# Two gate chunks in front of the first query pairs, and attention blocks two chunks later

## The chip, the cores and the metric

The kernel runs on one core of a Trainium2 chip. The metric is the device time of one execution in microseconds (us); the lower, the better. Engines are named as in the profile: PE (TensorE, the matmuls), DVE (VectorE), ACT (ScalarE), POOL (GpSimd) and SP (the queue that issues most DMAs).

## The reference

One decoder layer on 512 tokens of width 1024, in float32: a SwiGLU block, a mixer, and a second SwiGLU block, each between two RMS norms. The change lies in the mixer:

```
z = u @ w_in
gate_br, x_br, q, k, v, g_lru, g_attn = jnp.split(z, IN_SPLITS, axis=-1)
xc = causal_depthwise_conv(x_br, conv_w, conv_b)
y_lru = rg_lru(xc, ...) * jax.nn.gelu(gate_br)
q, k = apply_rope(q, cos, sin), apply_rope(k, cos, sin)
y_attn = sliding_window_attention_with_sinks(q, k, v, attn_sinks)
merged = sigmoid(g_lru) * (y_lru @ w_proj_lru) + sigmoid(g_attn) * (y_attn @ w_proj_attn)
return merged @ w_out
```

`rg_lru` computes two gates of `xc` by small block-diagonal matrices and then runs a linear recurrence along the tokens. Attention has 16 query heads in 4 groups, one key/value head for each group, and a window of 128 tokens, so a block of 128 queries sees 256 keys (128 in the first block).

## The kernel before, in words

Each float32 operand of a matmul is split into a rounded high part and the low remainder, and a product is three matmuls (`mm3`, lines 133 to 135): high by high, high by low, low by high. A chunk is 128 output columns for all 512 tokens over 8 steps of the inner dimension (`feat_chunk`), so 24 matmuls of 128x512.

Weights go through one pipeline in the order of the list `worder`, 84 pieces of 128x1024. `wload` issues a DMA on SP's queue into a `wraw` tile (line 96). `wsplit` casts it on ACT into the high half of a `w` tile (line 103) and has DVE subtract for the low half (line 104). `wget` hands out the next tile and first has everything up to two pieces further on split; a split issues the load of the piece three further on. `w` tiles come from the pool `big`, 19 slots of 128x2048 floats; `wraw` tiles and the attention scores come from a pool of 8.

The order of the instructions on each engine is the work of the framework's scheduler: it takes the program's order as priority and fills by its own estimate of times. What the kernel writes is therefore the priority, and engines then run their queues strictly in the planned order. Side work is written as generators: `start` runs one up to its first `yield n`, and each `tick()`, at the end of every chunk, counts down; after n ticks the generator goes on.

The mixer's first part runs in this order:

- `v_group` and `x_group(0)`, `k_pair`, `x_group(1)`: the recurrent branch's columns in two groups of four chunks. Each chunk starts `lru_chunk`: convolution on DVE (L907), and some ticks later the gate matmuls (tiles `r` and `i`), activations on ACT, and DVE's products. The last chunk of a group does the tail for all four: L929 (DVE), a square root on ACT (L930), and one tick apart for each chunk L933 (a product) and L934 (the scan along the tokens). The scans leave the recurrence's result in `lm`, which `hl` lists.
- Query pairs 0 and 1, `q_pair(0)` and `q_pair(1)`: two chunks each (`rope_pair`), then the rotary step: four products on DVE (L990), two sums on POOL (L991, L992), two casts on ACT (L996) and two subtractions on DVE (L997). One tick later the result goes to DRAM (L1015), another tick later it comes back in another layout as `qt` (L1020).
- Eight gate chunks, `gate_chunk(c)`: Square and Tanh on ACT (L1086, L1088), three passes on DVE (L1087, L1089, L1090, the last with `hl`), then the split into `ylh` and `yll` (L1092 on ACT, L1093 on DVE). Chunks 0 to 3 need the first group's recurrence, 4 to 7 the second's.
- Query pairs 2 and 3.

Attention is cut into blocks `attend(g, n)`, g the group of heads and n the block of queries. A block starts with the scores (tile `at..b`, L1036), DVE's masking (L1037), the maximum (L1042) and small operations (L1043 to L1052), exponentials on ACT (L1049), and POOL's scaling (L1053). Four ticks later come transposes (L1059), casts (L1061) and subtractions (L1062), two ticks after that the product with the values (L1069) and the write into `ya` (L1074). `next_attend` starts the next block of a list `todo`. The eight blocks of groups 0 and 1 are started one behind each of the gate chunks 2 to 7 (`ATT_GATES`) and one behind each of the two chunks of pair 2, through the argument `unit` of `rope_pair`.

After that follow eight steps of `sig_gate(c, yl, "gl")`, each a gate chunk (`glg`) and a projection chunk (`glp`), with the eight blocks of groups 2 and 3 started between them, and then the same for the attention branch (`gag`, `gap`) and the output projection.

Of the kernel before, what the change touches and what calls it, by code (L numbers as in the profile page):

```python
# [16 lines left out]
P = 128  # L17
# [2 lines left out]
TAIL = 7  # L20
JSTD = {"f1": 6, "f2": 4}
GC = 4
WARM = 8
LEAD = 3
PRODUCTS = (1, 2, 5, 6, 3, 7, 4)
FEATURE_LAG = {"b1": (4, 1), "b2": (3, 3, 3, 5)}
ATT_GATES = (2, 3, 4, 5, 6, 7)
T = 512
NT = T // P
D = 1024  # L30
KD = D // P
# [11 lines left out]
def hybrid_block_kernel(ctx, tc, x, xt, g1, w_first, gains, gu1, gs1, ds1, w_x, w_gate, w_q, w_k, w_v, w_gl, w_ga, w_pl, w_pa,  # L43
# [12 lines left out]
    def bank(name):  # L56
        return psum.tile([P, 512], F32, name=name, tag="bank")

    def t4(name, dtype=F32):
        return t4p.tile([P, 1024], dtype, name=name, tag="t4")  # L60

    def t2(name, dtype=F32):
        return t2p.tile([P, 512], dtype, name=name, tag="t2")

    def b8(name, shape, dtype=F32):
        return big.tile(shape, dtype, name=name, tag="b8")
# [4 lines left out]
    worder = []  # L71
    caps = []
    for gu in (gu1, gu2):
        worder += [gu[j, i] for j in range(gu.shape[0]) for i in range(2)]
        caps.append(len(worder))
        if gu is gu1:
            worder += [w_x[c] for c in range(4)] + [w_v[i] for i in range(2)] + [w_k[i] for i in range(2)]
            worder += [w_x[c] for c in range(4, 8)] + [w_q[i] for i in range(4)]
            worder += [w_gate[c] for c in range(8)] + [w_q[i] for i in range(4, 8)]
            worder += [w[c] for c in range(8) for w in (w_gl, w_pl)]  # L80
            worder += [w[c] for c in range(8) for w in (w_ga, w_pa)]
            worder += [w_o[c] for c in range(8)]
# [26 lines left out]
    def wget():  # L109
        i = wpos[0]  # L110
        wpos[0] += 1
        wsplit(i + 1 + AHEAD)
        return wready[i]
# [3 lines left out]
    def start(gen):  # L117
        n = next(gen, None)
        if n is not None:
            live.append([gen, n])  # L120

    def tick():
        for item in list(live):
            item[1] -= 1
            if item[1] <= 0:
                n = next(item[0], None)
                if n is None:
                    live.remove(item)
                else:
                    item[1] = n  # L130
# [22 lines left out]
    G.memset(idle.bitcast(F32), 0.0)  # L153
    for _ in range(WARM):
        PE.matmul(rb, lhsT=idle[:, :P], rhs=idle, start=True, stop=True)
# [21 lines left out]
    def feat_chunk(b, w, u, tok):  # L177
        wh, wl = w
        for k in range(KD):
            ks = slice(k * P, (k + 1) * P)  # L180
            mm3(b[:, tok], wh[:, ks], wl[:, ks], at(u, 0, k, tok), at(u, 1, k, tok), k == 0, k == KD - 1)
# [22 lines left out]
    def gate_up(u, name, first, fast, rs, ds, ending, also={}):  # L204
        ps = {}

        def pw(j):
            key = j // (2 * GC), j % 2
            if key not in ps:
                ps[key] = b8(f"{name}p{j}", [P, GC, T])  # L210
            return ps[key][:, j // 2 % GC, :]

# [179 lines left out]
    class Whole:  # L392
# [6 lines left out]
        def part(self, g, r, hi):  # L399
            n = GC if g < 2 else 3  # L400
            return self.ps[g, r][:, :n, 256:512] if hi else self.ps[g, r][:, :n, 0:256]
# [20 lines left out]
        def add_up(self, q):  # L422
# [4 lines left out]
            if s % 2 == 0 and i == 5:  # L427
                self.sums[g] = t4(f"{self.name}sum{g}").rearrange("p (c t) -> p c t", c=GC)[:, :GC if g < 2 else 3]
                self.sub(self.sums[g], self.part(g, 0, True), self.part(g, 1, True))
# [3 lines left out]
        def high(self, q):  # L433
# [9 lines left out]
            if s % 2 == 0:  # L443
                z = {1: (0, False), 2: (1, False), 3: (1, False), 4: (1, True), 7: (0, True)}.get(i)
                z = self.sums[g] if z is None else self.part(g, *z)
                a = b8(f"{self.name}a{i}{g}", [P, 2, GC, 256], F32R)[:, :, :GC if g < 2 else 3]
                self.a[i, g] = a, z
# [491 lines left out]
    def x_group(gi):  # L939
        a4, m4, bx4 = (b8(f"{n}{gi}", [P, 4, T]) for n in ("la", "lm", "lb"))  # L940
        hl.append(m4)
        cr = range(4 * gi, 4 * gi + 4)
        if gi == 0:
            first_four(u2, "x", lambda c, b: start(lru_chunk(c, b, a4, m4, bx4, c == cr[-1])), lambda: (next(vs), gates()))
        else:
            for c in cr:
                w = wget()
                b = bank(f"x{c}")
                feat_chunk(b, w, u2, ALL)
                tick()  # L950
                start(lru_chunk(c, b, a4, m4, bx4, c == cr[-1]))
# [26 lines left out]
    def rope_pair(name, unit=lambda: None):  # L978
        bs = []
        for i in range(2):  # L980
            w = wget()
            b = bank(f"{name}{i}")
            feat_chunk(b, w, u2, ALL)
            tick()
            unit()
            bs.append(b)
        ba, bb = bs
        m = [t2(f"{name}m{i}") for i in range(4)]
        for o, z, i in zip(m, (ba, ba, bb, bb), (0, 1, 0, 1)):
            V.tensor_tensor(out=o, in0=z, in1=cs[:, i, :], op=ALU.mult)  # L990
        G.tensor_tensor(out=m[0], in0=m[0], in1=m[3], op=ALU.subtract)  # L991
        G.tensor_tensor(out=m[2], in0=m[2], in1=m[1], op=ALU.add)  # L992
        st = b8(f"{name}st", [P, 4, T], F32R)
        for i, z in enumerate((m[0], m[2])):
            hi, lo = (st[:, 2 * i, :], st[:, 2 * i + 1, :]) if name == "kk" else (st[:, i, :], st[:, 2 + i, :])
            A.copy(hi, z)  # L996
            V.tensor_tensor(out=lo, in0=z, in1=hi.bitcast(F32), op=ALU.subtract)  # L997
        return st.bitcast(F32)
# [12 lines left out]
    def q_pair(m, unit=lambda: None):  # L1011
        st = rope_pair(f"q{m}", unit)
        yield 1
        dr = dram.tile([P, 4, T], F32, name=f"q_halves{m}")
        SP.dma_start(dr, st)  # L1015
        yield 1
        qt = b8(f"qt{m}", [P, 4, T], F32R)
        src = dr.rearrange("(i p) r t -> r p i t", i=4)
        for r in range(4):
            SP.dma_start(qt[32 * r:32 * r + 32].bitcast(F32), src[r])  # L1020
        qts[m] = qt
# [57 lines left out]
    def gate_chunk(c):  # L1079
        w = wget()  # L1080
        b = bank(f"gt{c}")
        feat_chunk(b, w, u2, ALL)
        if c % 4 == 0:
            yl.append((b8(f"ylh{c}", [P, 4, T], F32R), b8(f"yll{c}", [P, 4, T], F32R)))
        p = t2(f"gp{c}")
        A.activation(p, b, AF.Square)  # L1086
        V.scalar_tensor_tensor(out=p, in0=p, scalar=1.0 / GELU_C, in1=b, op0=ALU.add, op1=ALU.mult)  # L1087
        A.activation(p, p, AF.Tanh, scale=SQRT_2_PI * GELU_C)  # L1088
        V.scalar_tensor_tensor(out=p, in0=p, scalar=1.0, in1=b, op0=ALU.add, op1=ALU.mult)  # L1089
        V.scalar_tensor_tensor(out=p, in0=p, scalar=0.5, in1=hl[c // 4][:, c % 4, :], op0=ALU.mult, op1=ALU.mult)  # L1090
        yh, yo = yl[-1]
        A.copy(yh[:, c % 4, :], p)  # L1092
        V.tensor_tensor(out=yo[:, c % 4, :], in0=p, in1=yh[:, c % 4, :].bitcast(F32), op=ALU.subtract)  # L1093
        tick()
# [24 lines left out]
    kp = [b8(f"kp{i}", [P, 2, 2, T], F32R) for i in range(2)]  # L1119
    start(k_pair(kp))  # L1120
    x_group(1)
    for m in range(2):
        start(q_pair(m))
    y0 = b8("ya0", [P, 4, T])
    todo = [(g, n) for n in range(NT) for g in range(2)]

    def next_attend(*a):
        if todo:
            g, n = todo.pop(0)
            start(attend(g, n, kp, vt, y0 if g < 2 else y1))  # L1130

    for c in range(KD):
        gate_chunk(c)
        if c in ATT_GATES:
            next_attend()
    start(q_pair(2, next_attend))
    start(q_pair(3))
    y1 = b8("ya1", [P, 4, T])
    ya = []

    def split_y(src, name):
# [137 lines left out]
```

## Time and profile before

| | us |
|---|---|
| median of 3 runs | 1113.12 (1112.94 to 1113.57) |
| the profiled execution's own time | 1113.28 |
| its span, first to last instruction | 1111.5 |
| PE busy | 1099.9 |
| DVE busy | 898.4 |
| ACT busy | 597.2 |
| POOL busy | 97.9 |

The rows of the profile that are shown below give a line of the code, an engine, an operation and its tiles, written as output<-inputs with buffer numbers left out; then partitions x elements, how many there are, and times. In a timeline the first column is the start in us from the start of the span, the second the length, and brackets at the end give the time that the engine was idle just before and which instruction it then waited for. Rows of like instructions are merged. In a list of waits the numbers are us in total, times, and the longest.

### The profile page before, as it was taken

The page shows a single profiled execution, that of the slowest core. Times are in us where ns is not written, and L with a number is a line of the kernel's source. Part 1 is how long each engine was busy: PE and PEld are TensorE (multiplying, and loading weights), DVE is VectorE, ACT ScalarE, POOL GpSimd, SP SyncE. Part 2 cuts the span into 40 slices and gives each one's busy share as a digit, 9 for nine tenths or more (in the row PEclk, how much of TensorE's full clock was granted, in tenths as well). Part 3 has the DMA queues.
Part 4 walks back from the last instruction along what each step waited for, and adds up shares of the span by engine and source line. Part 5 has one row for each costly group of instructions (what it writes and reads, how often), then busy time and mean ns, then how long its engine had stood idle before and what let it go on. Part 6 is the DMA issues. An engine that isn't in the chain of part 4 may idle for free.

```text
span 1111.5 us, 16695 instructions
## 1 busy us (share of the span) xinstructions
PE 1099.9 (99%) x6550; PEld 981.5 (88%) x6550; DVE 898.4 (81%) x1266; ACT 597.2 (54%) x983; POOL 97.9 (9%) x100
## 2 busy tenths in 40 slices
PE   9999999999999999999999999999999999999997
PEld 7889999988889988787888888888999999998886
DVE  7999898889988799999777562546768889979877
ACT  7445554564665659567555351425435455457563
POOL 0000000012211011014022000000000000001310
PEclk9999999999999999999999999999999999999999
DMA  8223333498967264512822340533313333377973
GB/s 319 65 71 114 110 96 100 150 219 211 227 205 267 83 161 144 151 57 69 258 72 95 114 169 21 162 141 110 119 60 94 114 114 100 92 214 181 233 177 114
DMA packets 46079, 154.88 MB, mean 139 GB/s; under 512 B 5552, under 2 KB 5680, under 8 KB 45360
## 3 DMA queue, kind: packets, MB, share of 16 engines
q1 hardware_dynamic: 36496, 122.09, 34.4%
q0 software_dynamic: 6912, 23.07, 11.0%
q10 hardware_dynamic: 2592, 8.66, 2.1%
q8 instruction: 51, 0.84, 0.3%
q14 instruction: 28, 0.23, 0.1%
HBM read 142.26 MB, written 11.53 MB: 138 GB/s over the span
## 4 chain that ended last, share of the span: by engine, by line
PE 91%; DVE 7%; ACT 1%; issue 1%; DVEq 0%; POOL 0%; ACTq 0%; POOLq 0%
PE f2X L135 5%; PE f2X L134 5%; PE f2X L133 5%; PE f1X L135 5%; PE f1X L133 5%; PE f1X L134 5%; PE f1f L850 2%; PE f2Q L134 2%; PE f2Q L135 2%; PE f2Q L133 2%; PE f1Q L135 1%; PE f1Q L134 1%; PE f1Q L133 1%; PE glg L135 1%; PE glp L133 1%; PE glp L135 1%
## 5 line engine op out<-in xcount | busy, mean ns | idle before, releaser
L104 DVE TENSOR_TENSOR w<-wraw,w 128x1024 fp32r<-128x1024 f32 x84 | 104.2, 1274 | 16.8 <-ACT w L103 14.5
L103 ACT CAST w<-wraw 128x1024 fp32r<-128x1024 f32 x84 | 84.4, 1047 | 21.9 <-PE glp L135 6.0
L135 PE MATMUL f1X<-u1m,f1W 128*128 128x256 f32 x256 | 72.5, 283 | 0.0
L134 PE MATMUL f1X<-u1m,f1W 128*128 128x256 f32 x256 | 72.4, 283 | 0.0
L133 PE MATMUL f1X<-u1m,f1W 128*128 128x256 f32 x256 | 72.4, 283 | 0.0
L420 DVE TENSOR_TENSOR f2w<-f2b,f2w 128x1024 fp32r<-128x1024 f32 (+1 forms) x42 | 46.6, 1132 | 11.6 <-ACT f2w L442 11.6
L420 DVE TENSOR_TENSOR f1w<-f1b,f1w 128x1024 fp32r<-128x1024 f32 (+1 forms) x42 | 46.7, 1132 | 4.0 <-ACT f1w L442 4.0
L135 PEld LDWEIGHTS f1X<-u1m,f1W 128*128 128x128 f32 x256 | 49.1, 192 | 0.2 <-DVE f1W L275 0.2
L133 PEld LDWEIGHTS f1X<-u1m,f1W 128*128 128x128 f32 x256 | 49.1, 192 | 0.1
L134 PEld LDWEIGHTS f1X<-u1m,f1W 128*128 128x128 f32 x256 | 49.1, 192 | 0.1
L442 ACT CAST f1w<-f1b 128x1024 fp32r<-128x1024 f32 (+1 forms) x42 | 40.0, 979 | 11.5 <-PE f1Y L135 3.9
L442 ACT CAST f2w<-f2b 128x1024 fp32r<-128x1024 f32 (+1 forms) x42 | 39.8, 978 | 10.8 <-PE f2Y L135 3.9
L464 POOL DMA_DIRECT2D f1b<-in_ds_dram x24 | 20.9, 870 | 278.1 <-DVE f1w L420 270.1
L464 POOL DMA_DIRECT2D f2b<-in_ds_dram x24 | 20.9, 871 | 263.5 <-DVE f2w L420 261.1
L134 PE MATMUL f2Q<-u3m,f2W 128*128 128x256 f32 x144 | 40.8, 283 | 0.0
L134 PE MATMUL f2X<-u3m,f2W 128*128 128x256 f32 x144 | 40.8, 283 | 0.0
L135 PE MATMUL f2X<-u3m,f2W 128*128 128x256 f32 x144 | 40.8, 283 | 0.0
L135 PE MATMUL f2Q<-u3m,f2W 128*128 128x256 f32 x144 | 40.8, 283 | 0.0
L135 PE MATMUL f2X<-u3h,f2W 128*128 128x256 f32 x144 | 40.8, 283 | 0.0
L133 PE MATMUL f2Q<-u3m,f2W 128*128 128x256 f32 x144 | 40.8, 283 | 0.0
L134 PE MATMUL f2X<-u3l,f2W 128*128 128x256 f32 x144 | 40.8, 283 | 0.0
L133 PE MATMUL f2X<-u3m,f2W 128*128 128x256 f32 x144 | 40.7, 283 | 0.0
(809 smaller groups left out, 3946.7 us busy)
## 6 DMA issues: line engine op xcount, KB each, us to landing
f1b<-in_ds_dram POOLq DMA_DIRECT2D x20, 512.0 KB, 9.3
f2b<-in_ds_dram POOLq DMA_DIRECT2D x20, 512.0 KB, 9.4
f2L<-in_gs_dram SPq DMA_DIRECT2D x18, 512.0 KB, 3.5
f2R<-in_gs_dram SPq DMA_DIRECT2D x18, 512.0 KB, 4.4
wraw<-in_gu_dram SPq DMA_DIRECT2D x16, 512.0 KB, 5.7
f1L<-in_gs_dram SPq DMA_DIRECT2D x16, 512.0 KB, 3.5
f1R<-in_gs_dram SPq DMA_DIRECT2D x16, 512.0 KB, 4.4
f1b<-in_ds_dram SPq DMA_DIRECT2D x16, 512.0 KB, 5.0
```

The costliest lines, as they stand in the source:

```text
L103: A.copy(w[:, 0, :], raws[n])
L104: V.tensor_tensor(out=w[:, 1, :], in0=raws[n], in1=w[:, 0, :].bitcast(F32), op=ALU.subtract)
L133: PE.matmul(o, lhsT=ah, rhs=bh, start=start, stop=False, skip_group_check=reopen)
L134: PE.matmul(o, lhsT=ah, rhs=bl, start=False, stop=False, skip_group_check=reopen)
L135: PE.matmul(o, lhsT=al, rhs=bh, start=False, stop=stop, skip_group_check=reopen)
L420: V.tensor_tensor(out=o, in0=x0, in1=x1, op=ALU.subtract)
L442: A.copy(w[:, 0], self.w[i, s][1])
L464: G.dma_start(raw, self.ds[s, more][:, :n], accum_op=ALU.add)
L850: PE.matmul(bs[i], lhsT=lw[:, i * P:(i + 1) * P], rhs=rx, start=k == 0 and n == 0, stop=k == KD - 1 and n == 2)
```

## The change

The loop of gate chunks is cut in two. Chunks 0 and 1 (`GF = 2`) are computed right behind `x_group(1)`, ahead of the query pairs 0 and 1; the other six follow behind these pairs. The list of weights is reordered in the same way. Attention blocks now start behind the gate chunks 4 to 7 instead of 2 to 7, and behind all four chunks of the query pairs 2 and 3 instead of pair 2's two. The output tile `ya1` is created ahead of pair 2, and `ya0` ahead of the pairs 0 and 1.

```diff
+GF = 2
...
-            worder += [w_x[c] for c in range(4, 8)] + [w_q[i] for i in range(4)]
-            worder += [w_gate[c] for c in range(8)] + [w_q[i] for i in range(4, 8)]
+            worder += [w_x[c] for c in range(4, 8)] + [w_gate[c] for c in range(GF)] + [w_q[i] for i in range(4)]
+            worder += [w_gate[c] for c in range(GF, 8)] + [w_q[i] for i in range(4, 8)]
...
     x_group(1)
-    for m in range(2):
-        start(q_pair(m))
     y0 = b8("ya0", [P, 4, T])
...
-    for c in range(KD):
+    for c in range(GF):
         gate_chunk(c)
-        if c in ATT_GATES:
+    for m in range(2):
+        start(q_pair(m))
+    for c in range(GF, KD):
+        gate_chunk(c)
+        if c >= 4:
             next_attend()
+    y1 = b8("ya1", [P, 4, T])
     start(q_pair(2, next_attend))
-    start(q_pair(3))
-    y1 = b8("ya1", [P, 4, T])
+    start(q_pair(3, next_attend))
```

## The prediction

> **What bounds the kernel now.** The page's first part comes first, then TensorE's list of waits.
>
> ```profile
> PE 1099.9 (99%) x6550; PEld 981.5 (88%) x6550; DVE 898.4 (81%) x1266; ACT 597.2 (54%) x983; POOL 97.9 (9%) x100
> ...
> PE gt L135 <- DVE w L104: 1.5, 2, 0.8
> ...
> PE glg L133 <- ACT w L103: 1.2, 1, 1.2
> PE glg L135 <- DVE w L104: 0.5, 1, 0.5
> ```
>
> TensorE is busy in 1099.9 of 1111.5 us of span, and the change takes no matmul away. All that it can win are these four waits. Each is for a split weight tile `w`: ScalarE's cast of the high half (L103) or VectorE's subtraction for the low half (L104). So TensorE bounds the kernel, and in these places VectorE and ScalarE, as feeders, bound TensorE. I give the sixteen 128-column chunks behind `x_group(1)` numbers, C1 to C16. Before, C1 to C4 are the query pairs 0 and 1, C5 to C12 are the gate chunks 0 to 7, C13 to C16 the query pairs 2 and 3. The waits lie in C7 and C8 (gates 2 and 3) and in the first `gl` chunk behind C16, as TensorE's timeline shows (columns: start, length, then in brackets the idle time before).
>
> ```profile
> 452.52 0.39 PE L134 MATMUL gt<-b1ul,w 128*128 128x512 f32 x1
> 452.75 1.00 PE L1036 MATMUL at00b<-kp,qt 128*128 128x128 f32 x8
> 454.55 0.50 PE L135 MATMUL gt<-b1uh,w 128*128 128x512 f32 x1 [0.80 <-DVE w L104]
> 454.89 0.39 PE L133 MATMUL gt<-b1uh,w 128*128 128x512 f32 x1
> ...
> 459.44 0.39 PE L135 MATMUL gt<-b1uh,w 128*128 128x512 f32 x1
> 459.82 0.50 PE L133 MATMUL gt<-b1uh,w 128*128 128x512 f32 x1
> 460.15 0.40 PE L134 MATMUL gt<-b1ul,w 128*128 128x512 f32 x1
> 461.29 0.50 PE L135 MATMUL gt<-b1uh,w 128*128 128x512 f32 x1 [0.74 <-DVE w L104]
> ...
> 522.97 1.03 PE L1059 MATMUL at12t<-ident,at12s 128*128 128x128 f32 x8
> 525.21 0.50 PE L133 MATMUL glg<-b1uh,w 128*128 128x512 f32 x1 [1.20 <-ACT w L103]
> ...
> 526.70 0.60 PE L1059 MATMUL at03t<-ident,at03s 128*128 128x128 f32 x4
> 527.83 0.50 PE L135 MATMUL glg<-b1uh,w 128*128 128x512 f32 x1 [0.53 <-DVE w L104]
> ```
>
> Undisturbed, a 512-column matmul starts 0.23 us behind the last one (452.52 to 452.75). That makes the losses larger than the idle times: a matmul lasts 0.39, so 0.16 of it no longer overlaps the next one, and after a wait the next start takes 0.34 (454.55 to 454.89), 0.11 more. Loss 1: 0.80 + 0.16 + 0.11 = 1.05. Loss 2: 459.44 to 461.29 is three starts, 1.85 instead of 0.69, with the restart 1.25. Loss 3: 1.20 and 0.53, each with 0.27, 2.3. Together 4.6 us: that is the ceiling, 0.41%.
>
> **Why they happen.** The table by stretches, then the two feeders' timelines.
>
> ```profile
> 414.00:441.00 27.00, 27.00 (x121) 22.36 (x120) 24.53 (x33) 23.29 (x33) 3.00 (x2) 1.00 0.45 145
> 441.00:454.50 13.50, 12.75 (x61) 10.58 (x59) 12.71 (x15) 6.98 (x8) 3.09 (x2) 1.00 0.59 162
> 467.00:509.00 42.00, 42.00 (x222) 35.91 (x222) 39.33 (x73) 25.72 (x66) 5.41 (x5) 1.00 0.16 51
> 509.00:525.00 16.00, 15.01 (x77) 12.44 (x75) 15.03 (x29) 10.55 (x34) 9.42 (x6) 1.00 0.14 49
> 525.00:560.00 35.00, 34.26 (x169) 28.69 (x170) 28.39 (x44) 19.41 (x38) 5.28 (x4) 1.00 0.81 241
> ```
>
> Columns: stretch, length, then PE, PEld, DVE, ACT and POOL busy, the granted clock (1.00 throughout), DMA. VectorE is 91% busy in C1 to C4 (24.53 of 27), 94% in 441 to 454.5, 94% in 467 to 525 and 81% behind 525. So a weight's split waits behind whatever stands ahead of it on that queue.
>
> ```profile
> 444.10 3.60 DVE L933 TENSOR_TENSOR lb<-lb,lm 128x512 f32<-128x512 f32 x4 [0.79 <-ACT lm L930]
> 448.22 2.33 DVE L934 TENSOR_TENSOR_SCAN lm<-la,lb 128x512 f32<-128x512 f32 x2
> 451.06 2.33 DVE L934 TENSOR_TENSOR_SCAN lm<-la,lb 128x512 f32<-128x512 f32 x2
> 453.30 1.19 DVE L104 TENSOR_TENSOR w<-wraw,w 128x1024 fp32r<-128x1024 f32 x1
> ...
> 446.50 1.05 ACT L103 CAST w<-wraw 128x1024 fp32r<-128x1024 f32 x1
> 452.49 0.60 ACT L1086 ACTIVATE gp<-gt 128x512 f32<-128x512 f32 x1 [4.39 <-PE gt L135]
> 458.71 3.89 ACT L103 CAST w<-wraw 128x1024 fp32r<-128x1024 f32 x4
> ```
>
> Loss 1: the weight of C7 was cast by 447.55, but its subtraction ran at 453.30, behind the tail of the second recurrence (four L933, four scans). Loss 2: the weight of C8 was not cast until 458.71, in one burst with three others, behind the gate arithmetic of chunk 0, which the same tail had delayed.
>
> ```profile
> 514.27 1.28 DVE L990 TENSOR_TENSOR q2m<-q,cs 128x512 f32<-128x512 f32 x2
> 523.61 0.60 ACT L996 CAST q2st<-q2m 128x512 fp32r<-128x512 f32 x1
> 524.11 1.99 ACT L103 CAST w<-wraw 128x1024 fp32r<-128x1024 f32 x2
> 525.19 3.73 DVE L104 TENSOR_TENSOR w<-wraw,w 128x1024 fp32r<-128x1024 f32 x2 [0.24 <-ACT w L103]
> 524.54 2.16 POOL L1053 TENSOR_TENSOR at13s<-at13s,at13ss 128x1024 f32<-128x1024 f32 x1 [0.40 <-DVE at13ss L1052]
> ```
>
> Loss 3: the cast for the first `gl` chunk stands on ScalarE right behind the rotary cast of pair 2, whose multiplications VectorE only reached at 514.27 because it was full of attention work.
>
> **The change, part by part.** Prices for the moved work, from VectorE's groups by line, 454 to 525:
>
> ```profile
> L1087 DVE SCALAR_TENSOR_TENSOR gp<-gp,gt 128x512 f32<-128x512 f32 x8 | 5.3, 675 | 0.1
> L990 DVE TENSOR_TENSOR q2m<-q,cs 128x512 f32<-128x512 f32 x4 | 2.6, 681 | 0.0
> L1037 DVE SCALAR_TENSOR_TENSOR at12s<-at12b,msk 128x512 f32<-128x512 f32 x2 | 1.4, 676 | 0.0
> L1042 DVE TENSOR_REDUCE at12m<-at12s 128x4 f32<-128x1024 f32 x1 | 1.2, 1204 | 0.0
> L1062 DVE TENSOR_TENSOR at02pl<-at02t,at02ph 128x512 fp32r<-128x512 f32 x2 | 1.4, 676 | 0.0
> L1074 DVE TENSOR_TENSOR ya<-at00o,at00c 64x512 f32<-64x512 f32 x1 | 0.7, 676 | 0.0
> ```
>
> *Two gate chunks to C1 and C2; pairs 0 and 1 to C3 to C6.* Nothing is added. A gate chunk has four VectorE passes of the size of L1087, 2.7 us, so two have 5.4; a query pair has six of the size of L990 (four L990, two L997), 4.1. Up to the end of C4 VectorE thus gets 5.4 instead of pair 0's 4.1, 1.3 us more, inside the 2.5 us that it was idle between 414 and 441. ScalarE gets six passes (Square, Tanh, cast, twice) instead of two casts: four more at about 0.6 (row 452.49), 2.4 us against its 3.7 us idle. Both fit, but barely. I cost this at nothing; if the cover is gone, the weights of C3 to C6 come up to 1.3 us later than before.
>
> *The order of the weights and the DMA queue.* The load order follows the new order of use, with the same sixteen tiles. Pair 0's and pair 1's spills and reloads on SP's queue go two chunks later, past two weight loads. I cost them at nothing: the first attention block moves two chunks too, so what needs the queries moves along.
>
> *Slots.* `big` has 19. In C1 to C4 the change holds four `b1u` halves, `vt`, two `kp`, two `bd`, `lm0` and the second group's three, 13 by the code, and now also `ylh0`, `yll0` and perhaps `ya0`: 16, so three are left for weights instead of five or six. A weight is then cast only when the chunk before has freed its slot: 1.05 + 1.19 against a chunk of 24 starts at 0.23, 5.4 us. That is hidden, so nothing; uncovered it would be at most those 2.2 us, once.
>
> *Loss 1 in C7.* The recurrence's tail is tied to ticks behind `x_group(1)`, which do not move, and C7's weight is again gate 2's, its split again issued at the start of C5, behind a rotary pair (pair 0 instead of 1). I expect the same burst and the subtraction again ending at 454.50. But no attention matmul is then there to fill the wait: TensorE would have gone on at 452.75, and loses 1.8 and a restart, 1.9, so 0.85 more. Ends: 0 if the split gets ahead of the scans (1.05 won), and 3.2 if VectorE's extra 1.3 us all arrive there (2.15 lost). I take 1.9, nearest to the row at 453.30.
>
> *Loss 2 in C8.* Gate arithmetic of chunks 0 and 1 is over by then, so C8's cast has only the rotary pair beside it, and attention's first block no longer stands there. I take all of loss 2 away, 1.25 won; ends 0 and 1.25.
>
> *Loss 3 behind C16.* Attention now starts in C9 instead of C7. Its eight blocks cost VectorE 1.35, 1.2, 1.35 and 0.7, about 4.6 us each without the small operations. When the first `gl` weight's split is issued (start of C15), six blocks have been begun instead of eight: up to 9.2 us less ahead of it. The lateness is a cast that came 1.4 us late, so I take loss 3 away, 2.3 won. Ends: 2.3 won, and 1.4 lost on top of loss 3 if another split meets a long GpSimd multiply: at 525.19 two subtractions took 3.73, where twice the 1.19 of row 453.30 is 2.4, while L1053 ran on GpSimd at 524.54. [...]
>
> *What is late next.* The two blocks in C15 and C16 push 9.2 us of VectorE work towards 525 to 560, which had 35.0 - 28.4 = 6.6 us idle. 2.6 us do not fit there and run on into the later `gl` chunks, in front of the blocks of heads 2 and 3; I cost that at nothing as long as splits go first.
>
> Sum against the profiled execution's own 1113.28 us (span 1111.5): +0.85 - 1.25 - 2.3 = -2.7, so 1110.6. The median of the runs shown, 1113.12, is 0.16 lower, so I leave 1110.5.
>
> **The rivals.** *All three losses go.* The planner, with two chunks less of gate arithmetic in its heap at 447, puts the subtraction ahead of the scans. For it: the tile was cast six microseconds earlier. Against it: nothing else in the rows shows VectorE leaving the recurrence for a split. 1113.1 - 4.6 = 1108.5.
>
> *Attention's load only moves (no real change).* Attention is as dense as before, eight blocks in eight chunks, and ends at C16 with pair 3 behind it; the first `gl` cast keeps its place behind a rotary cast and loss 3 stays. For it: ScalarE's order at 523.61 and 524.11. Against it: the 9.2 us. 1113.1 + 0.85 - 1.25 = 1112.7.
>
> *Slower: the `gl` stage starves.* The 2.6 us that do not fit behind 525 hold up the splits of `gl` and `pl` 0 and 1, in program order behind blocks 6 and 7 and pair 3. Loss 3 stays and grows by those 2.6: 1113.1 + 0.85 - 1.25 + 2.6 = 1115.3. It decides if VectorE is over 94% busy to about 540. Against it: splits go ahead of attention in priority, and only in-order traps delay them.
>
> **How the numbers follow.** Chances: forecast 0.42, own range 1109.2 to 1111.8 (half of loss 1 or loss 3 either way); all gone 0.16; only moved 0.28; slower 0.14. A change of 0.2%, 2.2 us, is about what can be told from none: the borders are 1110.9 and 1115.3. Six tenths of the forecast's case lies under 1110.9, with all of the first rival: 0.25 + 0.16, and 0.02 of the second, 0.43 faster. Slower: the last rival, whose mid-point lies on the border, gives 0.07, and starvation in C3 to C6 with the other ends of loss 1 and loss 3 together 0.06: 0.13. The rest, 0.44, is within. Range 1108.4 to 1114.5: it leaves out most of the slower rival and a sliver below.
>
> **What would show it.** Right: no TensorE wait in C8, none over 0.5 us in the first `gl` chunk, one of 1.5 to 2 us in C7 on L104, VectorE over 90% from 470 to 535. Wrong: L104 of gate 2 ahead of the scans (then faster); waits of `glg` or `glp` on L103 or L104 between 520 and 560 (then no gain); waits on weights in C3 to C6, which would say that the cover of the early gates was too thin.

## The result and the profile after

The changed kernel takes 1117.51 us (median of 6 executions, 1116.72 to 1118.56), the kernel before 1113.12 on the same chip: a ratio of 1.0042, 95% interval 1.0032 to 1.0052, so 4.4 us (0.4%) slower. The profiled execution took 1116.88 with a span of 1115.1.

The first line of the page, and TensorE's waits from 440 to 560 us in the changed kernel (us in total, times, longest). Line numbers from 24 on are one higher than before (L105 is the split, L104 the cast):

```profile
PE 1101.2 (99%) x6550; PEld 983.0 (88%) x6550; DVE 897.1 (80%) x1266; ACT 596.8 (54%) x983; POOL 97.5 (9%) x100
...
PE gt L136 <- DVE w L105: 2.9, 1, 2.9
PE at13b L1037 <- DVE at03s L1038: 2.5, 1, 2.5
PE glg L136 <- DVE w L105: 0.3, 1, 0.3
```

The number of matmuls is the same. Four waits of 3.2 us in all have become three of 5.7, and the two long ones cost more than they last. TensorE's timeline of the changed kernel around them:

```profile
451.90 0.39 PE L135 MATMUL gt<-b1ul,w 128*128 128x512 f32 x1
455.15 0.79 PE L136 MATMUL gt<-b1uh,w 128*128 128x512 f32 x1 [2.86 <-DVE w L105]
455.74 0.63 PE L134 MATMUL gt<-b1uh,w 128*128 128x512 f32 x1
456.17 0.63 PE L135 MATMUL gt<-b1ul,w 128*128 128x512 f32 x1
...
519.59 1.03 PE L1060 MATMUL at11t<-ident,at11s 128*128 128x128 f32 x8
523.10 2.07 PE L1037 MATMUL at13b<-kp,qt 128*128 128x256 f32 x8 [2.48 <-DVE at03s L1038]
524.97 0.63 PE L134 MATMUL glg<-b1uh,w 128*128 128x512 f32 x1
525.40 0.63 PE L135 MATMUL glg<-b1ul,w 128*128 128x512 f32 x1
```

Behind each wait the 512-column matmuls start 0.43 us apart (455.74 to 456.17, 524.97 to 525.40) where they start 0.23 apart ahead of the first (451.22 to 451.45), for about 3 us. The table by stretches names the reason in its third column from the right, the granted clock; its first columns are the stretch, its length and TensorE's busy time:

```profile
449.00:455.00 6.00, 3.29 (x15) 2.40 (x13) 6.00 (x7) 0.00 (x0) 0.00 (x0) 0.98 0.43 175
455.00:458.50 3.50, 3.35 (x9) 2.68 (x10) 2.43 (x4) 0.24 (x1) 1.54 (x2) 0.55 0.65 195
...
520.00:523.00 3.00, 0.62 (x6) 0.38 (x4) 3.00 (x5) 2.31 (x5) 0.00 (x0) 1.00 0.72 292
523.00:526.50 3.50, 3.40 (x12) 3.11 (x13) 3.44 (x6) 0.00 (x0) 0.00 (x0) 0.51 0.83 231
```

The clock is 0.55 and 0.51 in the 3.5 us behind each wait, and VectorE is busy right through both waits (6.00 of 6, 3.00 of 3). At its lowest, 0.50, it stands from 454.73 to 458.14 and from 522.99 to 526.40, 3.41 us each. Counted from start to start, the place in C7 costs 4.5 us (before 1.1) and the place behind C16 4.3, and another 0.8 in the small wait at 542 (before 2.5 for the whole place). Loss 2 in C8, 1.3, is gone. The sum +3.4 + 2.6 - 1.3 is 4.7. In the two profiled executions the first 20 us, which no edit touches, went the other way by 1.1, which leaves the 3.6 between the spans.

**What VectorE did during the two waits.** First C7, VectorE's timeline and the row of ScalarE's cast:

```profile
443.50 3.59 DVE L934 TENSOR_TENSOR lb<-lb,lm 128x512 f32<-128x512 f32 x4 [0.79 <-ACT lm L931]
...
450.45 1.21 DVE L935 TENSOR_TENSOR_SCAN lm<-la,lb 128x512 f32<-128x512 f32 x1
451.59 1.26 DVE L991 TENSOR_TENSOR q1m<-q,cs 128x512 f32<-128x512 f32 x2
452.76 1.21 DVE L935 TENSOR_TENSOR_SCAN lm<-la,lb 128x512 f32<-128x512 f32 x1
453.90 2.33 DVE L105 TENSOR_TENSOR w<-wraw,w 128x1024 fp32r<-128x1024 f32 x2
...
445.90 2.00 ACT L104 CAST w<-wraw 128x1024 fp32r<-128x1024 f32 x2
```

Gate 2's weight was cast by 447 (the row of ScalarE holds two weights and ends at 447.90), and its subtraction stands behind the tail as before, now with two of pair 1's products (451.59) between the scans as well. TensorE kept to its order meanwhile: the matmuls of 455.74 and 456.17 need only the high half, cast by 447, and ran behind the wait of 2.86 us. Behind C16, VectorE, then POOL, then ScalarE's cast, and as the last row VectorE in the kernel before:

```profile
512.08 0.92 DVE L1044 TENSOR_TENSOR at12m<-at12m,sink 128x4 f32<-128x4 f32 x1
513.10 1.15 DVE L1046 TENSOR_TENSOR at12e<-sink,at12m 128x4 f32<-128x4 f32 x1
...
516.67 0.16 DVE L1052 TENSOR_TENSOR at12ss<-at12ss,at12e 128x4 f32<-128x4 f32 x1 [1.63 <-ACT at12s L1050]
517.18 0.69 DVE L998 TENSOR_TENSOR q2st<-q2m,q2st 128x512 fp32r<-128x512 f32 x1
...
518.40 1.78 DVE L998 TENSOR_TENSOR q2st<-q2m,q2st 128x512 fp32r<-128x512 f32 x1
520.10 2.35 DVE L105 TENSOR_TENSOR w<-wraw,w 128x1024 fp32r<-128x1024 f32 x2
522.37 1.28 DVE L1038 SCALAR_TENSOR_TENSOR at03s<-at03b,msk 128x512 f32<-128x512 f32 x2
...
511.70 1.28 POOL L993 TENSOR_TENSOR q2m<-q2m,q2m 128x512 f32<-128x512 f32 x1 [0.49 <-DVE q2m L991]
512.93 1.30 POOL L992 TENSOR_TENSOR q2m<-q2m,q2m 128x512 f32<-128x512 f32 x1
517.21 2.41 POOL L1054 TENSOR_TENSOR at12s<-at12s,at12ss 128x1024 f32<-128x1024 f32 x1 [2.98 <-ACT q2st L997]
...
518.17 2.00 ACT L104 CAST w<-wraw 128x1024 fp32r<-128x1024 f32 x2
...
502.75 0.65 DVE L1037 SCALAR_TENSOR_TENSOR at03s<-at03b,msk 128x512 f32<-128x512 f32 x1
```

TensorE waits for the mask pass of at03 at 522.37, which reads at03's scores out of their PSUM banks (the accumulators that matmuls write into; the kernel has a pool of eight). Block at13 uses nothing of at03, so what it waits for can only be such a bank. Ahead of the mask pass three things add up. Two operations on four numbers a row take 0.92 and 1.15 us: they end at 513.00 and 514.25, where POOL's two rotary sums end at 512.98 and 514.23. The exponentials of at12 start behind them, at 514.55, and VectorE then stands idle for 1.63 us until 516.67, because the next instruction in its order needs their sum. And of three subtractions beside POOL's multiply (517.21 to 519.62) the last, a rotary one, takes 1.78 us, 1.09 more than the two ahead of it, 0.69 each at 517.18 and 517.79.

The holds, as I call these longer times beside POOL, are not new: in the kernel before, two such operations of at13 take 0.88 and 1.14 us at 518.32 and 519.31, beside the same two sums. But there at03's mask pass was done by 503.40 (the last row), long ahead of pair 2's products at 514.27. What the change brought is that the mask pass stands behind them.

### The profile page after: what moved, and what is told of

The parts are those of the page before. It is cut to its first block, busy times and chain, and to the rows that moved or that the text cites. A ratio compares the mean times of both kernels' runs of the same rounds, so it can differ in the third digit from the quotient of the medians.

```text
span 1115.1 us, 16698 instructions
## 1 busy us (share of the span) xinstructions
PE 1101.2 (99%) x6550; PEld 983.0 (88%) x6550; DVE 897.1 (80%) x1266; ACT 596.8 (54%) x983; POOL 97.5 (9%) x100
## 4 chain that ended last, share of the span: by engine, by line
PE 90%; DVE 7%; ACT 2%; issue 1%; DVEq 0%; POOL 0%; ACTq 0%; POOLq 0%
PE f2X L134 5%; PE f2X L136 5%; PE f2X L135 5%; PE f1X L136 5%; PE f1X L135 5%; PE f1X L134 5%; PE f1f L851 2%; PE f2Q L136 2%; PE f2Q L135 2%; PE f2Q L134 2%; PE f1Q L136 1%; PE f1Q L135 1%; PE f1Q L134 1%; PE glg L136 1%; PE glg L134 1%; PE glg L135 1%
## 5 line engine op out<-in xcount | busy, mean ns | idle before, releaser
L105 DVE TENSOR_TENSOR w<-wraw,w 128x1024 fp32r<-128x1024 f32 x84 | 103.0, 1260 | 12.3 <-ACT w L104 11.1
L104 ACT CAST w<-wraw 128x1024 fp32r<-128x1024 f32 x84 | 84.7, 1047 | 17.4 <-PE glp L136 4.6
```

The source lines that it names most:

```text
L104: A.copy(w[:, 0, :], raws[n])
L105: V.tensor_tensor(out=w[:, 1, :], in0=raws[n], in1=w[:, 0, :].bitcast(F32), op=ALU.subtract)
```

## The experiments

Fourteen kernels, each timed in five rounds beside the kernel before. Theory A at the start: two places, gate 2's split behind the recurrence's tail, and the last attention block's scores behind a late mask pass.

**1. The change's two halves.** The gate half alone: the changed kernel with attention started as before.

```diff
-        if c >= 4:
+        if c in ATT_GATES:
...
-    start(q_pair(3, next_attend))
+    start(q_pair(3))
```

> Half of the change: gate chunks 0 and 1 ahead of the query pairs 0 and 1, attention blocks where they were before (behind the gate chunks 2 to 7 and pair 2's two chunks). Theory A (the time lies in two new TensorE waits, one for each half of the change, each followed by some microseconds at half clock): only the first wait is here, for gate chunk 2's split weight, about 3.0 us of wait and 1.5 us at half clock, and loss 3 stays as before (2.3), so 1113.1 + 4.5 + 2.3 - 4.6 = 1115.3 us. Rival B (the halves are harmless alone, and it is attention starting later that does all the harm): no longer than before, 1113 us or less. Rival C (the early gates do all of it): 1117 us or more.

Measured: 1123.87 us, ratio 1.0099 (1.0085 to 1.0113). TensorE's waits in it:

```profile
PE at10b L1037 <- DMA qt<-q_halves: 5.5, 1, 5.5
PE gt L136 <- DVE w L105: 3.3, 1, 3.3
```

Theory A missed this by 8.6 us: pair 1 now runs two chunks later, its queries are not back from DRAM when block at10 starts, and TensorE waits 5.5 us for them, with a half-rate stretch behind, as an estimate from the run's mean clock: that is 0.993, where the 6.82 us at 0.50 in gate 2 alone, taken off the 0.999 of before, leave 0.996. Rival C's bound of 1117 holds, but for another cause. Here the wait of 3.3 us in gate 2 is followed by twice the stretch of the changed kernel: the clock is 0.50 for 6.82 us (454.90 to 461.72; the matmuls start 0.43 us apart from 456.39 to 461.51), which costs some 2.7 us instead of 1.5. The attention half alone, as an edit of the changed kernel: gates, pairs and the list of weights in the old order (the list and `GF` are not shown), attention as in the change.

```diff
+    for m in range(2):
+        start(q_pair(m))
     y0 = b8("ya0", [P, 4, T])
...
-    for c in range(GF):
-        gate_chunk(c)
-    for m in range(2):
-        start(q_pair(m))
-    for c in range(GF, KD):
+    for c in range(KD):
```

> The other half: query pairs 0 and 1 first as before, attention blocks behind gate chunks 4 to 7 and all four chunks of pairs 2 and 3. Theory A: the score matmuls of the last block (at13b) wait for a PSUM bank that VectorE's mask pass of block at03 has yet to read, 2.6 us and 1.6 us at half clock; in gate chunk 2 the wait of before without its attention matmuls, 1.9; loss 2 gone: 1113.1 + 4.2 + 1.9 - 4.6 = 1114.6 us. Rival B (attention later does all the harm): 1117 us or more. Rival C (the early gates do all of it): 1113 us or less.

Measured: 1114.67, ratio 1.0017 (1.0008 to 1.0026), as theory A had it. Its waits, and its stretches around them:

```profile
PE at13b L1036 <- DVE at03s L1037: 2.0, 1, 2.0
PE gt L135 <- DVE w L104: 1.6, 1, 1.6
...
455.00:458.50 3.50, 3.50 (x17) 2.90 (x16) 3.33 (x6) 2.62 (x5) 0.00 (x0) 1.00 0.97 231
...
519.00:522.50 3.50, 1.73 (x9) 1.68 (x10) 3.47 (x5) 1.03 (x2) 0.00 (x0) 0.87 0.97 344
522.50:526.50 4.00, 4.00 (x14) 3.14 (x14) 3.97 (x7) 0.00 (x0) 0.00 (x0) 0.69 0.86 214
```

Both new losses are there without the early gates: taking the attention blocks out of C7 leaves gate 2's wait uncovered (1.6), and putting two into pair 3 makes the wait at at13b. The early gates add pair 1's products in front of the split, and the wait goes from 1.6 to 2.9. Here the wait of 1.6 us leaves the clock at 1.00, and the one of 2.0 lowers it (0.87 and 0.69).

**2. Is the half-rate stretch caused by the idle time?** Ten matmuls whose result nobody reads, put in front of gate 2's wait:

```diff
+                for _ in range(fill):
+                    PE.matmul(spare, lhsT=wh[:, ks], rhs=ah, start=True, stop=True)
...
-        feat_chunk(b, w, u2, ALL)
+        feat_chunk(b, w, u2, ALL, 10 if c == 2 else 0)
```

> The whole change, and ten dummy matmuls of 128x512 (2.3 us) into a spare PSUM bank in gate chunk 2, right where TensorE waits 2.9 us for the split weight. Nothing becomes ready earlier. Theory A (the wait makes the clock drop, and the 1.5 us behind it are that drop): the restart runs at full rate, 1117.5 - 1.5 = 1116.0 us, matmuls behind the wait 0.23 us apart. Rival D (the slow restart has nothing to do with TensorE's idleness, say operands that arrive slowly): matmuls still 0.43 us apart, 1117.5 us.

Measured: 1116.56, ratio 1.0032 (1.0020 to 1.0043), with an interval that does not separate the two theories. The timeline does:

```profile
451.98 2.43 PE L188 MATMUL spare<-b1uh,w 128*128 128x512 f32 x10
...
455.44 0.50 PE L189 MATMUL gt<-b1uh,w 128*128 128x512 f32 x1 [0.57 <-DVE w L105]
455.77 0.40 PE L134 MATMUL gt<-b1uh,w 128*128 128x512 f32 x1
456.01 0.39 PE L135 MATMUL gt<-b1ul,w 128*128 128x512 f32 x1
```

With TensorE kept busy the same split comes no earlier (455.44), and the matmuls behind it run at once at 0.23, at a clock of 1.00 from 455 to 458.5 where it was 0.55. So the half rate belongs to the idle time. A new wait of 0.8 us at at30b took part of the gain. A wait of 2.0 us was enough for it (experiment 1), and the stretches at 0.50 lasted 3.41 us or twice that, 6.82; what sets these lengths was not shown.

**3. The recurrence's tail out of gate 2's way.** The tail of gate group 1 two chunks later:

```diff
-        yield LRU_LAG[c // 4]
+        yield LRU_LAG[c // 4] + (2 if c == 7 else 0)
```

> The whole change, with the gate matmuls of the recurrence's last chunk two ticks later (lag 5 instead of 3), so that VectorE's order has the splits for gate chunks 2 and 3 ahead of the tail of products and scans. Theory A: the wait in gate chunk 2 goes with its half-clock stretch, the one at at13b stays: 1117.5 - 4.5 = 1113.0 us. Rival E (VectorE has simply too much to do there, whatever the order): the wait only moves to the next chunks, 1116 us or more.

Measured: 1113.96, ratio 1.0013 (1.0004 to 1.0021). VectorE's timeline and TensorE's waits:

```profile
448.30 2.35 DVE L105 TENSOR_TENSOR w<-wraw,w 128x1024 fp32r<-128x1024 f32 x2
450.72 2.50 DVE L934 TENSOR_TENSOR lb<-lb,lm 128x512 f32<-128x512 f32 x4
...
PE at13b L1037 <- DVE at03s L1038: 3.7, 1, 3.7
```

The splits now run at 448.30, ahead of the tail, and gate 2 does not wait: that cause is shown. Expected was 1113.0, the 4.5 us that C7 lost; 3.5 were won, since the wait at at13b grew from 2.5 to 3.7: it begins 4.4 us sooner than in the changed kernel and ends only 3.2 sooner, because VectorE has not gained as much as TensorE.

**4. Is it the place of block at13?** One block fewer in pair 3, left to the `gl` stage (and `ya0`'s split two chunks later):

```diff
-    start(q_pair(3, next_attend))
+    start(q_pair(3, lambda: len(todo) > 1 and next_attend()))
...
-        if c == 2:
+        if c == 4:
             start(split_y(y0, "ya0"))
```

> The changed kernel with one block fewer started in front of the gl stage: the last of the eight blocks on the first two query pairs (at13) is left to the gl stage's own calls, and the split of the attention output ya0 is started two gl chunks later to fit. Theory A (TensorE takes its work in order, so a block's scores that wait for a bank which VectorE has not read yet hold up the gl chunk behind them; VectorE is some 3 us behind there because of pair 2's rotary products, the POOL holds and the two first weight splits of the gl stage): the wait of 2.5 us at at13b and the half-rate matmuls behind it (4.3 us together in the stretch from 520 to 540) are gone, the wait of 2.9 us in gate 2 stays as it is: 1117.5 - 4.2 = 1113.3 us. Rival R (VectorE simply has too much work in this stretch, so whatever stands there next waits as long): a wait of 2 us or more appears at the first gl chunk or at the block that follows, 1116.5 or more.

Measured: 1116.76, ratio 1.0036 (1.0023 to 1.0050). Theory A failed here; TensorE's timeline:

```profile
520.01 1.03 PE L1060 MATMUL at11t<-ident,at11s 128*128 128x128 f32 x8
523.62 0.47 PE L134 MATMUL glg<-b1uh,w 128*128 128x512 f32 x1 [2.57 <-DVE at03s L1038]
```

Without at13 the `gl` chunk itself waits, for the same mask pass and as long. So not the block in front, but the lateness of at03's mask is the cause. With the later tail added,

> The changed kernel with both repairs: the tail of gate group 1's recurrence two chunks later (lag 5 in place of 3 for chunk 7), and the last block at13 left to the gl stage. Theory A: neither gate 2 nor at13b waits; what is left of the 11.9 us of start-to-start loss of the changed kernel is that less 4.5 and 4.3: 1117.5 - 8.6 = 1109 us (1108 to 1110.5), under both kernels by 4 us against before. Rival R (the work that is put off comes back as a wait in the gl stage): 1112.5 or more.

the same again: 1113.87, ratio 1.0009 (1.0001 to 1.0018), and the `gl` chunk waits 3.8 us for at03's mask. The rival had it.

**5. The tail alone in the kernel before.** The edit of 3 in the kernel before:

> The kernel before with one edit: the tail of gate group 1's recurrence two chunks later (lag 5 in place of 3 for chunk 7). Theory A (the two waits for split weights in gates 2 and 3, 1.05 and 1.25 us, were the recurrence's tail in front of the splits on VectorE): both gone, the gl stage's first weight wait of 2.3 us stays: 1113.1 - 2.3 = 1110.8 us. Rival R (the tail stands in front of something as urgent two chunks on): 1112.5 or more.

Measured: 1111.69, ratio 0.9991 (0.9982 to 0.9999). That is between the two expectations. Losses 1 and 2 (2.3 us) are gone, but 1.6 us came back in a new place, the wait of the first row; the waits for the first `gl` weight went from 1.2 and 0.5 to 0.8 and 0.5:

```profile
PE at10t L1059 <- POOL at10s L1053: 1.5, 1, 1.5
PE glg L133 <- ACT w L103: 0.8, 1, 0.8
PE glg L135 <- DVE w L104: 0.5, 1, 0.5
```

**6. POOL's passes ahead of the late mask.** Theory A1: they make it late. Left out are pair 2's two rotary sums and the normalising of at12:

```diff
+        if name != "q2":
             G.tensor_tensor(out=m[0], in0=m[0], in1=m[3], op=ALU.subtract)
             G.tensor_tensor(out=m[2], in0=m[2], in1=m[1], op=ALU.add)
...
+        if nm != "at12":
             G.tensor_tensor(out=s, in0=s, in1=ss.rearrange("p (h o) -> p h o", o=1).broadcast_to([P, 4, W]), op=ALU.mult)
```

> The changed kernel without three POOL passes just ahead of the at13b wait: the two rotary sums of query pair 2 and the normalising of block at12 are left out (the result is not the reference's). Theory A1 (VectorE's mask pass for at03 is late because those POOL passes hold up its two-input operations: 0.92 and 1.15 us for two operations on four numbers a row that take 0.16 us elsewhere, 1.78 instead of 0.69 for a subtraction, some 2.9 us): the wait of 2.5 us at at13b falls under 0.5 and the half-rate matmuls behind it go too: 1113.3 us. Rival A2 (the mask pass is late by the amount of VectorE's own work and the order that it is given, with or without POOL): the wait stays at 1.5 us or more, and the time at 1116 or more.

Measured: 1112.52, ratio 0.9998 (0.9989 to 1.0007). The wait behind C16 is gone altogether, that in gate 2 (2.8) is the only one left. With the later tail as well,

> The changed kernel with the tail two chunks later, and pair 2's two POOL sums and block at12's normalising left out (the result is not the reference's). If the two waits are the whole of what the change costs and each of the two causes is its own: 1112.5 (the POOL passes left out alone) less the 4.2 us lost in gate 2 = 1108.3 us, and no wait over 1 us from the first gate to the gl stage. Rival: TensorE, not held in gate 2, arrives 3 us sooner than VectorE can follow, and a wait of 1 us or more comes back in front of the gl stage: 1109.5 to 1111.5.

1108.65, ratio 0.9964 (0.9951 to 0.9977). The only wait left between 440 and 620 us is one of 0.8 us in the `gl` stage. Against the changed kernel that is 8.9 us won, as much as the two places cost (4.5 and 4.3): they are the whole loss. Leaving out the POOL passes takes away their holds and whatever in VectorE's order waited for them, so this does not yet say which of the two it was.

**7. An order that avoids it?** Blocks begun one chunk sooner, with the later tail:

```diff
-        if c >= 4:
+        if c >= 3:
             next_attend()
```

> The changed kernel with the tail of gate group 1's recurrence two chunks later, and the attention blocks begun one chunk sooner (behind the fourth gate chunk in place of the fifth), so that the last of the eight stands behind the first chunk of query pair 3 and the second chunk has none. Theory B (all eight banks hold results that VectorE has not read, because at03's mask pass stands in VectorE's order behind pair 2's rotary products, their POOL sums and the two weight splits): with at03 a chunk earlier its mask pass comes ahead of the rotary products, and the wait of 3.7 us and the half-rate stretch behind it (5.7 to 6.1 us together in the run with the tail alone, 1114.0) are gone: 1109 us (1108 to 1111), under both kernels. Rival R1 (the stretch has too much VectorE work in whatever order): a wait of 2 us or more at at13b or at the gl stage, 1112.5 or more. Rival R2: pair 0's queries are not there yet for the first block, a DMA wait, 1115 or more.

Measured: 1118.10, ratio 1.0043 (1.0029 to 1.0057): rival R2, though with the other pair, `at10b` waiting 5.7 us for pair 1's reload. The mask pass of at03 now runs from 512.74, ahead of pair 2's products at 516.93, and the wait at at13b is gone, as theory B said (TensorE, held up before, also gets there later). But the queries allow no earlier start, not even by one chunk.

**8. The sums on VectorE.** Nothing left out, pair 2's sums moved off POOL, with the later tail:

```diff
+        E = V if name == "q2" else G
-        G.tensor_tensor(out=m[0], in0=m[0], in1=m[3], op=ALU.subtract)
-        G.tensor_tensor(out=m[2], in0=m[2], in1=m[1], op=ALU.add)
+        E.tensor_tensor(out=m[0], in0=m[0], in1=m[3], op=ALU.subtract)
+        E.tensor_tensor(out=m[2], in0=m[2], in1=m[1], op=ALU.add)
```

> The changed kernel with the tail two chunks later, and pair 2's two rotary sums on VectorE in place of POOL. Theory B with the POOL hold (those sums held VectorE's two small two-input operations for 0.77 and 1.0 us; on VectorE they take some 0.65 us each): VectorE comes out 0.5 us ahead, the wait at at13b goes from 3.7 to 3.2, 1113.4 us. Rival (no hold: VectorE simply gets 1.3 us more): the wait grows to 5 us, 1115.3.

Measured: 1109.40, ratio 0.9975 (0.9964 to 0.9986). The direction was right and the size 4 us short. VectorE's timeline (one line number higher again than in the changed kernel):

```profile
508.86 0.14 DVE L1045 TENSOR_TENSOR at12m<-at12m,sink 128x4 f32<-128x4 f32 x1
508.93 0.67 DVE L994 TENSOR_TENSOR q2m<-q2m,q2m 128x512 f32<-128x512 f32 x1
509.54 0.67 DVE L993 TENSOR_TENSOR q2m<-q2m,q2m 128x512 f32<-128x512 f32 x1
510.14 0.14 DVE L1047 TENSOR_TENSOR at12e<-sink,at12m 128x4 f32<-128x4 f32 x1
...
512.08 0.67 DVE L999 TENSOR_TENSOR q2st<-q2m,q2st 128x512 fp32r<-128x512 f32 x1
...
515.55 1.27 DVE L1039 SCALAR_TENSOR_TENSOR at03s<-at03b,msk 128x512 f32<-128x512 f32 x2
516.75 0.14 DVE L1053 TENSOR_TENSOR at12ss<-at12ss,at12e 128x4 f32<-128x4 f32 x1
```

VectorE does 1.2 us more and reaches the mask at 515.55. Counted from the first small operation of at12, that is 6.7 us, against 10.3 in the changed kernel (512.08 to 522.37). The expectation had counted only the two small operations (0.77 and 1.0). The held subtraction is undisturbed too (0.67), and VectorE never stands idle for the exponentials, because at12's sum now stands behind the mask. How much of that is the holds and how much the order of instructions that came with them, these runs do not separate.

The same edit without the later tail:

> The changed kernel with pair 2's rotary sums on VectorE and nothing else. If those POOL passes and what they put VectorE in order behind are the whole cause of the at13b wait: that wait and the half-rate matmuls behind it go, 4.2 us, the wait in gate 2 stays: 1113.3 us, all of the computation kept. Rival (the sums bring that only together with the later tail): a wait of 1.5 us or more stays at at13b, 1116 or more.

Measured: 1112.99, ratio 1.0004 (0.9995 to 1.0013), as expected. TensorE waits 2.8 us in gate 2, as before the edit, and for at03's mask not at all. The same for pair 3, with the later tail:

> The changed kernel with the tail two chunks later and the rotary sums of pairs 2 and 3 both on VectorE. In the 1109.4 run the second gl chunk waits 1.3 us for a split that stands behind the same pattern at pair 3 (two small operations of 0.88 and 1.14 us beside POOL's sums, 1.63 us idle for the exponentials, a subtraction of 1.77 beside POOL's normalising). If the pattern is the cause, that wait goes: 1109.4 - 1.3 = 1108.1 us. Rival (VectorE has too much to do there): the wait stays or grows, 1109.4 or more.

Measured: 1108.92, ratio 0.9965 (0.9952 to 0.9977). TensorE has no wait between 440 and 620 us. This version computes everything and is faster than both kernels, by 0.35% against the kernel before.

**9. Is the change worth anything once repaired?** The kernel before with the later tail and pair 2's sums on VectorE:

> The kernel before with the two repairs that brought the changed kernel to 1109.4: the recurrence's tail two chunks later, and pair 2's rotary sums on VectorE. If the change's own gain is real (its order fills the waits that the old order has in front of the gl stage and at at10), the old order keeps those: 1111.7 with the tail alone, less at most 0.7 of the second gl wait, 1111.0 to 1111.7. Rival (the repairs bring all of it and the change nothing): 1109.4.

Measured: 1110.05, ratio 0.9976 (0.9966 to 0.9986), against 0.9975 (0.9964 to 0.9986) for the change with the same two edits. Its only wait from 440 to 560 us is the 1.5 of at10t from experiment 5. The two waits at the start of the `gl` stage went too, where the expectation had allowed 0.7 us at most. The time lies between the two expectations, nearer to the rival's: no gain of the change itself can be told from zero.

## Why the prediction was wrong

The forecast was 1110.5 us, by +0.85 - 1.25 - 2.3. By its steps:

- *Loss 1 in C7*: the mechanism was right and the size off. The forecast took 1.9 us, with an end of 3.2; the place lost 4.5. Two parts were missing. Two of pair 1's products stand between the scans, so that the subtraction starts 10.4 us behind the start of the tail (443.50 to 453.90) instead of 9.2 (444.10 to 453.30): these 1.2 us make a loss of 3.0 out of 1.8, close to the end of 3.2, which had put the extra at 1.3. And the clock costs 1.5 of the 4.5, of which that end knew nothing.
- *Loss 2 in C8*: right, gone in the changed kernel.
- *Loss 3 behind C16*: this step failed, and with the largest term. The weight did come in time, as forecast: the casts ran at 518.17, and the first `gl` chunk waits for no split, not in experiment 8 either, where nothing holds TensorE up in front of it. The step asked only whether a weight is late and did not ask what else TensorE needs, a free bank. Moving attention two chunks later puts at03's mask pass behind pair 2's rotary step, its POOL sums and the splits; experiment 4 (the same wait without at13) and experiment 8 (no wait once the sums leave POOL) show that chain, and not a weight, to be the cause. The forecast had this place lose nothing, 2.3 us won; it lost 4.3, and 0.8 more at 542.
- *POOL's hold*: the row was read rightly as a price against the change, but laid on the splits of the `gl` stage (1.4 us at most). It fell on three operations of at12 and pair 2. Experiments 6 and 8 show that the wait goes when the POOL passes go; how much of it is the holds and how much the order of instructions stays open.
- *The order of the weights and the DMA queue*: nothing, right, and the reason given is shown by experiments 1 and 7: attention begun two chunks sooner makes TensorE wait 5.5 us, and one chunk sooner 5.7, for the queries' reload.
- *Early gates at no cost, slots*: right; there are no weight waits in C3 to C6.
- *What is late next*: the 2.6 us of VectorE work were costed at nothing "as long as splits go first". Splits did go first, and that was the trap: the mask pass stood behind two of them. The slower rival had the direction and came within 2.2 us, but by starved splits.
- *The clock* stood in no step, because before shows 1.00 throughout from 414 to 560; the longest wait there is 1.2 us. It makes 1.5 and 1.6 us of the two places, 3.1 us beside a total of 4.4.

## What to carry to other kernels

Do not price a longer wait on TensorE at its length alone: here waits of 2.0 to 3.8 us brought half-rate matmuls with them, some 1.5 us in the changed kernel and 2.7 behind the 3.3 us wait of experiment 1, while those of 1.5 and 1.6 us (experiments 5 and 1), and the shorter ones between 440 and 560 us in the kernel before, left the clock at 1.00. So a wait that grows past the longest one in the profile of before can have a step in its cost. When work is moved later, ask for every reader that it now stands behind, the readers that free accumulators as well as those that feed weights, and remove the cause on the late engine instead of rearranging TensorE. And test a repair on the kernel before as well: here two small edits of VectorE's queue brought the gain in the old order just as well.

## What was not expected of the hardware

- The granted clock fell to 0.50 for 3.41 us after waits of 2.5 and 2.9 us, and it fell after one of 2.0 (0.87 over 3.5 us, then 0.69 over 4.0; by estimate some 3.4 us at 0.50, since the two together lack 1.7 us of full clock). After one of 3.3 us it stayed at 0.50 for 6.82. It stayed at 1.00 after one of 1.6.
- Operations on four numbers a row, 0.14 to 0.16 us by themselves, took 0.92 and 1.15 us beside POOL's sums. Two such holds delayed ScalarE's exponentials, and through them left VectorE idle for 1.63 us. By these rows, as an estimate, small operations at the head of a chain carried 3.4 us (0.77 + 1.0 + 1.63), and the held subtraction 1.09. Two sums cost 1.28 and 1.30 us on POOL, and 0.67 each on VectorE.
